# Two-layer streaming trunk with PEER experts: the operands of the gate products change places

## The chip, the cores and the metric

The kernel runs on one core of a Trainium2 chip. The metric is the device time of one execution of the whole program in microseconds; for the kernel before, the median of three runs is 2138.87 us (2137.55 to 2143.28).

The engines named below: PE (TensorE) does the matrix products, a product being a load of weights (the stationary operand) and a MATMUL that streams the moving operand past them into PSUM; DVE (VectorE), ACT (ScalarE) and POOL (GpSimd) work element by element; SP issues the transfers. Each engine has a queue of its own and works through it in order.

## The reference

Two request groups, 256 prompt tokens and 32 sample tokens of width 1024, go through two layers (an RG-LRU block, then a Conformer convolution block). Each layer is followed by a PEER mixer, which is where most of the time goes:

```
q  = h @ w_q                               # 8 heads x 2 halves of 128
s1, s2 = q[..., :half] @ k1.T, q[..., half:] @ k2.T      # 128 keys each
top 16 of s1, top 16 of s2, top 16 of their 256 sums per head
e  = idx1 * 128 + idx2                     # expert, of 16384
g  = softmax(sv)                           # 16 weights per head
z  = gelu(u[e] . h)
out = sum over heads and k of  g * z * v[e]
```

So every token has 8 x 16 = 128 chosen experts, each with a gate weight g.

## The kernel before

For the prompt tokens the kernel does not gather expert rows. It computes z for all 16384 experts with dense products (the up stage, 128 **z items** of 128 experts each), multiplies by a gate matrix that is zero for experts not chosen, and multiplies by all of v (the down stage, 128 v items). One item is one **step** of the stream `run_stream`. The 32 sample tokens do gather their rows, in threads that run beside these stages (`s_up`, L970, and `s_down`, L995).

**A z item** (`z_item`, L922) has these parts, each issued in a fixed step: four transfers load the expert rows (`load`, L925); DVE transposes them in blocks (`prep`, L933, the instruction is L935, two buffers `ut`), two steps ahead; ACT rounds to fp32r (hi, L332) and POOL subtracts for the remainder (lo, L333), one step ahead; PE does 24 products of 256 moving columns (`mm3`, L342), 16 with hi as weights and 8 with lo; a step later, for every second item, ACT applies gelu (L956, or L958 for tokens whose gates are there already, followed on DVE by the multiplication L959). The results go to `gz`, with the expert's low index on the partitions and items by tokens along the rows.

**The gate matrix** of a token is built as a sum of one-hot products. The 128 slots (head, k) of a token lie on the partitions. Slot s contributes its gate at place (idx2, idx1), so the matrix is `onehot(idx2).T @ (onehot(idx1) * g)`. The fp32 gate is split into its power of two (`sexp`) and its mantissa, and the mantissa into two f16 parts (`pmant`, in PSUM, as are the indices `pidx`), so that 16-bit products give the full value.

`gate_ops(g)` (L870) does this for four tokens at a time, 64 **groups** a layer. Its parts:

- `eq` (L878), on DVE: two compares with a ramp (L880, L881) make the one-hot rows `b4` (of idx2) and `one` (of idx1), and two multiplications (L882, L883) make `hi` and `lo` from `one`. All these tiles are 128 x 512 with the four tokens innermost: the row of token j is every fourth element.
- `exps` (L885), on ACT: four scalings (L887) multiply the row of each token in `b4` by its power of two, in place.
- `mm` (L889), on PE: for each token two products (L893), weights `b4[:, :, j]`, moving `hi[:, :, j]` and then `lo[:, :, j]`, summed in one PSUM bank for the four tokens.
- `ev` (L896): DVE multiplies the z values that are there already by the gates (L901), and ACT copies the gates for the items still to come (L904; L906 on DVE for the last few).

**What sets the order.** There is no scheduler: instructions go into the queues in the order in which the program issues them. After the products of each item, `run_threads` (L183) goes through the live threads in order of their start. An operation has a hop, its fourth entry: how many steps after the operation before it, at the least, it may be issued. For a group `eq` and `exps` are issued in the same step, `mm` one step later, `ev` another step later. A "Q" lets one group begin in each step, and a condition keeps a group from starting until the products of the group three before are issued. `hi`, `lo` and `b4` have three sets that groups take in turn, `one` has two. All lie in one scratch tile, `scr`, cut by `four(i, dt)` (L867) into pieces of 256 words. Pieces 0 and 1 held the indices and mantissas on their way to PSUM, and are free by then.

Of the kernel before, what the change touches and what calls it, by code (L numbers as in the profile page):

```python
# [11 lines left out]
F16 = mybir.dt.float16  # L12
BF16 = mybir.dt.bfloat16
I32 = mybir.dt.int32
U32 = mybir.dt.uint32
AF = mybir.ActivationFunctionType
ALU = mybir.AluOpType
# [4 lines left out]
P = 128  # L22
D = 1024
C = 8
NP = 256
# [21 lines left out]
def trunk_kernel(ctx: ExitStack, tc: tile.TileContext, I: dict, O: list):  # L47
    nc = tc.nc
    ctx.enter_context(tc.manual_schedule())
    V, S, G, TE = nc.vector, nc.scalar, nc.gpsimd, nc.tensor  # L50
# [14 lines left out]
    scr = bigp.tile([P, NSCR], F32, name="scr")  # L65
# [6 lines left out]
    def bank(acc=False):  # L72
        if acc:
            return psA.tile([P, 512], F32, tag="acc", name="acc")
        return psB.tile([P, 512], F32, tag="b", name="b")
# [520 lines left out]
    iota4 = scr[:, 3 * NP:4 * NP].bitcast(F16).rearrange("p (i t) -> p i t", t=4)  # L596
    sexp = scr[:, 2 * NP:3 * NP]
# [7 lines left out]
    def peer_items(l, st, x8, sq8, hT8, hp8, rep8, ada_list):  # L605
# [261 lines left out]
        def four(i, dt):  # L867
            return scr[:, i * NP:(i + 1) * NP].bitcast(dt).rearrange("p (i t) -> p i t", t=4)

        def gate_ops(g):  # L870
            t0 = 4 * g
            hi, lo, b4 = [four(4 + 3 * (g % 3) + i, dt) for i, dt in enumerate((F16, F16, BF16))]
            one = four(13 + g % 2, F16)
            tok = slice(t0, t0 + 4)
            s = {}
            row = lambda a: a.unsqueeze(1).to_broadcast([P, P, 4])

            def eq():  # L878
                idx, mant = st["pidx"], st["pmant"]
                V.tensor_tensor(b4, iota4, row(idx[:, 1, tok]), op=ALU.is_equal)  # L880
                V.tensor_tensor(one, iota4, row(idx[:, 0, tok]), op=ALU.is_equal)  # L881
                V.tensor_tensor(hi, one, row(mant[:, 0, tok]), op=ALU.mult)  # L882
                V.tensor_tensor(lo, one, row(mant[:, 1, tok]), op=ALU.mult)  # L883

            def exps():  # L885
                for j in range(4):
                    S.activation(b4[:, :, j], b4[:, :, j], AF.Copy, scale=sexp[:, t0 + j:t0 + j + 1])  # L887

            def mm():  # L889
                s["ps"] = bank(True)  # L890
                for j in range(4):
                    for a in (hi, lo):
                        TE.matmul(s["ps"][:, j * P:(j + 1) * P], b4[:, :, j], a[:, :, j], start=a is hi, stop=a is lo)  # L893
                st["nm"] += 1

            def ev():  # L896
                nz = st["nz"]
                assert st["nt"] == t0
                src = s["ps"].rearrange("p (t i) -> p i t", t=4)
                if nz:  # L900
                    V.tensor_tensor(gz[:, :nz, t0:t0 + 4], gz[:, :nz, t0:t0 + 4], src[:, :nz], op=ALU.mult)  # L901
                if nz < ET:
                    if ET - nz > 10:
                        last.append(lambda: S.copy(gz[:, nz:, t0:t0 + 4], src[:, nz:]))  # L904
                    else:
                        V.tensor_copy(gz[:, nz:, t0:t0 + 4], src[:, nz:])  # L906
                st["nt"] = t0 + 4
                if t0 == NP - 4:
                    for j in range(NS):
                        threads.append(Thread(s_up(j), group=("up%d" % l, 2)))  # L910
            return [("C", 0, lambda: st["nm"] >= g - 2), ("Q", 0, None), ("X", 0, eq, 0), ("X", 0, exps, 0),
                    ("X", 0, mm, 1), ("X", 0, ev, 1)]

        def start_gates():
            for g in range(NP // 4):
                threads.append(Thread(gate_ops(g), group=("gate%d" % l, 5)))
# [53 lines left out]
        def s_up(s):  # L970
            gt = scr[:, (s % 2) * D:(s % 2 + 1) * D]

            def ga():
                if s == 0:
                    nc.sync.dma_start(hs_v, hsave)
                G.indirect_dma_start(out=gt, out_offset=None, in_=Uf,  # L976
                                     in_offset=bass.IndirectOffsetOnAxis(ap=eidx[:, s:s + 1], axis=0))

            def dot():
                V.scalar_tensor_tensor(gt, gt, 1.0, hs_v, op0=ALU.mult, op1=ALU.mult, accum_out=zs[:, s:s + 1])  # L980
            ops = [("R", 1.6, None), ("G", 0.1, ga), ("V", 1.3, dot, 2)]
            if s == NS - 1:
                def act():
                    S.activation(zs, zs, AF.Gelu_apprx_tanh)

                def mid():
                    V.tensor_tensor(zs, zs, gsel, op=ALU.mult)
                    V.tensor_tensor(lz, dmask.unsqueeze(1).to_broadcast([P, NS, NS]),
                                    zs.unsqueeze(2).to_broadcast([P, NS, NS]), op=ALU.mult)
                    for j in range(0, NS, 2):  # L990
                        threads.append(Thread(s_down(j), group=("down%d" % l, 2)))
                ops += [("S", 0.2, act, 2), ("V", 1.4, mid, 2)]
            return ops
# [901 lines left out]
```

## Time and profile before

| | |
|---|---|
| median of 3 runs | 2138.87 us |
| profiled execution, its time | 2135.33 us |
| its span, first to last instruction | 2133.2 us |
| mean granted TensorE clock | 0.989 |
| gate groups of layer 0, about | 431.5 to 671.7 us |
| gate groups of layer 1, about | 1483.6 to 1723.7 us |

A row of the groups of instructions reads: line, engine, operation, written tile <- read tiles, shapes, count | busy us, mean ns of one | idle time of the engine ahead of them, and what ended it. "PEld" are PE's weight loads, which overlap with its products. A row of the waits reads: engine and line that waited <- engine and line waited for: us in all, times, the longest. A row of the stretches reads: the stretch, its length, then for each engine busy us and the number of instructions, the granted clock, the share of the transfer engines in use and the rate. A row of the order of time reads: start, duration from the first start to the last end, engine, line, count.

### The profile page before, as it was taken

Reading aid. Unit: us, or ns where it says so; the run is one execution under the profiler, and the core shown is the slowest. Engines: PE = TensorE matmul, PEld = TensorE weight load, DVE = VectorE, ACT = ScalarE, POOL = GpSimd, SP = SyncE. Lnnn points to the kernel's source line nnn. Section 1 sums busy time; section 2 is a strip of 40 time slices with the busy share of each in tenths; the row PEclk is TensorE's granted clock in tenths of the full one; section 3 lists DMA queues with packets and bytes.
Section 4 is the critical chain, followed back from the end, with each engine's and each line's share of the span. In section 5 each row is a group of like instructions: output and inputs, shape, how many; then the busy total and the mean of one; then the engine's idle time right before and its main releaser. Section 6 shows DMA issues by size and latency. Waiting matters only on the chain.

```text
span 2133.2 us, 38012 instructions
## 1 busy us (share of the span) xinstructions
PE 2048.1 (96%) x13603; PEld 1772.8 (83%) x13603; DVE 1550.8 (73%) x3316; ACT 1127.2 (53%) x1975; POOL 1000.4 (47%) x649
## 2 busy tenths in 40 slices
PE   7988999999999999999999899999999999999997
PEld 4777979999999788777876689989999997777776
DVE  4786569888888787455668755898888887765455
ACT  3654434477776444344443544445877754444444
POOL 4346667856666332110245366877666653211201
PEclk9999999999999999999999999999999999999999
DMA  9756585644445888886676545555444478888863
GB/s 337 261 184 208 153 237 164 179 134 144 139 139 174 304 310 298 283 277 229 237 262 146 169 143 158 173 159 169 148 139 139 134 236 302 296 278 294 277 199 121
DMA packets 311483, 444.44 MB, mean 208 GB/s; under 512 B 29326, under 2 KB 248126, under 8 KB 310782
## 3 DMA queue, kind: packets, MB, share of 16 engines
q1 hardware_dynamic: 292142, 374.73, 55.8%
q0 software_dynamic: 18976, 67.22, 9.0%
q8 instruction: 107, 1.75, 0.4%
q14 instruction: 82, 0.67, 0.1%
q10 hardware_dynamic: 176, 0.07, 0.0%
HBM read 434.19 MB, written 4.87 MB: 206 GB/s over the span
## 4 chain that ended last, share of the span: by engine, by line
PE 70%; DVE 13%; DMA 6%; issue 4%; POOL 4%; ACT 2%; SPq 1%; DVEq 0%; ACTq 0%; POOLq 0%
PE b L342 31%; PE acc L1069 27%; PE acc L893 5%; DVE ut L935 3%; POOL lo L333 3%; DMA raw<-in_peer_v_dram 2%; DMA raw<-in_peer_u_dram 2%; PE b L1013 1%; ACT hi L332 1%; DVE lo L333 1%; PE acc L406 1%; POOL scr L976 1%; DMA scr<-in_peer_u_dram,eidx 1%; PE b L695 1%; PE b L1689 1%
## 5 line engine op out<-in xcount | busy, mean ns | idle before, releaser
L342 PE MATMUL b<-rnd,hi 128*128 128x256 f32 (+1 forms) x5376 | 741.1, 290 | 19.2 <-ACT hi L332 8.4
L333 POOL TENSOR_TENSOR lo<-ut,hi 128x1024 fp32r<-128x1024 f32 x252 | 606.0, 2408 | 287.2 <-ACT hi L332 231.9
L342 PEld LDWEIGHTS b<-rnd,hi 128*128 128x128 f32 x5376 | 684.1, 190 | 43.4 <-ACT hi L332 15.2
L332 ACT CAST hi<-raw 128x1024 fp32r<-128x1024 f32 x336 | 353.1, 1052 | 397.0 <-DMA raw<-in_peer_v_dram 240.5
L1069 PE MATMUL acc<-hi,rnd 128*128 128x512 f32 x2048 | 557.7, 394 | 5.0 <-ACT hi L332 4.8
L333 DVE TENSOR_TENSOR lo<-raw,hi 128x1024 fp32r<-128x1024 f32 x282 | 348.1, 1238 | 257.2 <-PE acc L1069 127.8
L1069 PEld LDWEIGHTS acc<-hi,rnd 128*128 128x128 f32 x2048 | 380.3, 188 | 114.0 <-issue 22.5
L935 DVE STREAM_TRANSPOSE ut<-raw 128x1024 f32<-128x1024 f32 x256 | 317.3, 1240 | 187.8 <-POOL lo L333 93.7
L342 PE MATMUL b<-rnd,lo 128*128 128x256 f32 (+1 forms) x2688 | 387.3, 286 | 12.1 <-POOL lo L333 6.2
L342 PEld LDWEIGHTS b<-rnd,lo 128*128 128x128 f32 x2688 | 351.4, 189 | 17.8 <-POOL lo L333 10.1
L332 ACT CAST hi<-ut 128x1024 fp32r<-128x1024 f32 x256 | 268.4, 1048 | 159.8 <-DVE ut L935 139.2
L1069 PE MATMUL acc<-lo,rnd 128*128 128x512 f32 x1024 | 318.0, 391 | 1.1 <-DVE lo L333 0.8
L887 ACT ACTIVATE scr<-scr 128x128 bf16<-128x128 bf16 x512 | 192.2, 572 | 124.5 <-DVE scr L880 124.5
L1069 PEld LDWEIGHTS acc<-lo,rnd 128*128 128x128 f32 x1024 | 191.0, 188 | 46.4 <-DVE lo L333 6.7
L1003 POOL DMA_INDIRECT big<-in_peer_v_dram,eidx x64 | 62.1, 970 | 271.7 <-PE b L1013 258.6
L333 POOL TENSOR_TENSOR lo<-raw,hi 128x1024 fp32r<-128x1024 f32 x54 | 130.4, 2418 | 114.8 <-PE b L342 59.0
L976 POOL DMA_INDIRECT scr<-in_peer_u_dram,eidx x64 | 86.6, 1353 | 183.4 <-DVE scr L980 182.6
L893 PE MATMUL acc<-scr 128*128 128x128 f16 x1024 | 142.5, 296 | 2.6 <-DVE scr L882 2.5
L893 PEld LDWEIGHTS <-scr 128*128 128x128 bf16 x1024 | 104.1, 118 | 9.8 <-ACT scr L887 3.0
L980 DVE SCALAR_TENSOR_TENSOR scr<-scr 128x1024 f32<-128x1024 f32 x64 | 78.2, 1222 | 36.7 <-DMA scr<-in_peer_u_dram,eidx 35.9
L1044 DVE TENSOR_TENSOR rnd<-big,rnd 128x512 fp32r<-128x512 f32 x128 | 89.9, 702 | 5.5 <-ACT rnd L1043 5.5
L1043 ACT CAST rnd<-big 128x512 fp32r<-128x512 f32 x128 | 78.7, 615 | 5.5 <-PE b L342 5.5
(316 smaller groups left out, 1625.8 us busy)
## 6 DMA issues: line engine op xcount, KB each, us to landing
raw<-in_peer_u_dram SPq DMA_DIRECT2D x1024, 128.0 KB
raw<-in_peer_v_dram SPq DMA_DIRECT2D x256, 512.0 KB
big<-in_ada_w_dram SPq DMA_DIRECT2D x96, 512.0 KB
raw<-in_peer_w_q_dram SPq DMA_DIRECT2D x128, 128.0 KB
raw<-in_cf_w_pw_dram SPq DMA_DIRECT2D x24, 512.0 KB
raw<-in_lru_w_in_dram SPq DMA_DIRECT2D x16, 512.0 KB
raw<-in_lru_w_out_dram SPq DMA_DIRECT2D x8, 512.0 KB
xsave<-big SPq DMA_DIRECT2D x2, 1152.0 KB
```

The costliest lines, as they stand in the source:

```text
L332: S.copy(hi, src)
L333: (G if pool_lo else V).tensor_tensor(lo, src, hi.bitcast(F32), op=ALU.subtract)
L342: TE.matmul(ps, w[wi][:, c * P:(c + 1) * P], a[ai][:, c, :n], start=(start and wi == c == ai == 0), stop=(stop and wi == 1 and c == C - 1))
L887: S.activation(b4[:, :, j], b4[:, :, j], AF.Copy, scale=sexp[:, t0 + j:t0 + j + 1])
L893: TE.matmul(s["ps"][:, j * P:(j + 1) * P], b4[:, :, j], a[:, :, j], start=a is hi, stop=a is lo)
L935: V.transpose(s["ut"].rearrange("p (b e n) -> p e b n", b=8, e=4), s["raw"].rearrange("p (e b n) -> p e b n", e=4, b=8))
L976: G.indirect_dma_start(out=gt, out_offset=None, in_=Uf, in_offset=bass.IndirectOffsetOnAxis(ap=eidx[:, s:s + 1], axis=0))
L980: V.scalar_tensor_tensor(gt, gt, 1.0, hs_v, op0=ALU.mult, op1=ALU.mult, accum_out=zs[:, s:s + 1])
L1003: G.indirect_dma_start(out=gt[j], out_offset=None, in_=Vf, in_offset=bass.IndirectOffsetOnAxis(ap=eidx[:, s + j:s + j + 1], axis=0))
L1043: S.copy(w[0], src)
L1044: V.tensor_tensor(w[1], src, w[0].bitcast(F32), op=ALU.subtract)
L1069: TE.matmul(acc[tt][half], w[a][:, c0:c0 + P], s["w"][b][:, half * 512:(half + 1) * 512], start=(i == 0 and a == 0 and b == 0), stop=(i == ...
```

## The change

In the gate products the two operands change places, and with them the index that each one-hot row stands for, so that the result has the same layout. `b4` is now the one-hot rows of idx1 and `one` those of idx2; `hi` and `lo` (f16, every fourth element) become the weights. The scalings no longer work in place: they read `b4`, still every fourth element, and write a tile `bt` that has the four tokens outermost, so that the row of a token is 128 adjacent bf16 elements; these are the moving operand. `b4` goes to two sets in pieces 0 and 1 of the scratch, `bt` has three sets in pieces 10 to 12. `exps` gets a hop of 1: the scalings of a group are issued one step after its compares, and its products and their use follow a step later than before.

```diff
         def gate_ops(g):
             t0 = 4 * g
-            hi, lo, b4 = [four(4 + 3 * (g % 3) + i, dt) for i, dt in enumerate((F16, F16, BF16))]
+            hi, lo = [four(4 + 2 * (g % 3) + i, F16) for i in range(2)]
+
+            b4 = four(g % 2, BF16)
+            bt = scr[:, (10 + g % 3) * NP:(11 + g % 3) * NP].bitcast(BF16).rearrange("p (t i) -> p t i", t=4)
             one = four(13 + g % 2, F16)
...
             def eq():
                 idx, mant = st["pidx"], st["pmant"]
-                V.tensor_tensor(b4, iota4, row(idx[:, 1, tok]), op=ALU.is_equal)
-                V.tensor_tensor(one, iota4, row(idx[:, 0, tok]), op=ALU.is_equal)
+                V.tensor_tensor(b4, iota4, row(idx[:, 0, tok]), op=ALU.is_equal)
+                V.tensor_tensor(one, iota4, row(idx[:, 1, tok]), op=ALU.is_equal)
                 V.tensor_tensor(hi, one, row(mant[:, 0, tok]), op=ALU.mult)
                 V.tensor_tensor(lo, one, row(mant[:, 1, tok]), op=ALU.mult)
 
             def exps():
                 for j in range(4):
-                    S.activation(b4[:, :, j], b4[:, :, j], AF.Copy, scale=sexp[:, t0 + j:t0 + j + 1])
+                    S.activation(bt[:, j], b4[:, :, j], AF.Copy, scale=sexp[:, t0 + j:t0 + j + 1])
 
             def mm():
                 s["ps"] = bank(True)
                 for j in range(4):
                     for a in (hi, lo):
-                        TE.matmul(s["ps"][:, j * P:(j + 1) * P], b4[:, :, j], a[:, :, j], start=a is hi, stop=a is lo)
+                        TE.matmul(s["ps"][:, j * P:(j + 1) * P], a[:, :, j], bt[:, j], start=a is hi, stop=a is lo)
                 st["nm"] += 1
...
-            return [("C", 0, lambda: st["nm"] >= g - 2), ("Q", 0, None), ("X", 0, eq, 0), ("X", 0, exps, 0),
+            return [("C", 0, lambda: st["nm"] >= g - 2), ("Q", 0, None), ("X", 0, eq, 0), ("X", 0, exps, 1),
                     ("X", 0, mm, 1), ("X", 0, ev, 1)]
```

## The prediction

> **What bounds the kernel now.** I read the page's busy times and chain first, then the stretches in which the gate products run, then who waits for whom in them, and last the order of time of single instructions.
>
> ```profile
> PE 2048.1 (96%) x13603; PEld 1772.8 (83%) x13603; DVE 1550.8 (73%) x3316; ACT 1127.2 (53%) x1975; POOL 1000.4 (47%) x649
> PE 70%; DVE 13%; DMA 6%; issue 4%; POOL 4%; ACT 2%; SPq 1%; DVEq 0%; ACTq 0%; POOLq 0%
> ```
>
> TensorE carries 70% of the chain. 96% is an average over stages, so here are the two stretches that hold the gate products (layer 0, layer 1), and of the first one its beginning and its end:
>
> ```profile
> core 0: us, PE busy (x) PEld busy (x) DVE busy (x) ACT busy (x) POOL busy (x), PEclk, DMA share, GB/s
> 431.50:671.70 240.20, 239.41 (x2017) 235.37 (x2018) 206.03 (x416) 183.12 (x442) 152.20 (x64) 1.00 0.47 141
> 431.50:465.50 34.00, 33.21 (x275) 32.17 (x276) 27.74 (x60) 27.74 (x66) 21.65 (x9) 1.00 0.48 147
> 636.00:671.70 35.70, 35.70 (x304) 35.16 (x303) 32.24 (x64) 24.45 (x60) 21.34 (x10) 1.00 0.45 134
> 1483.60:1723.70 240.10, 239.39 (x2017) 235.31 (x2017) 206.19 (x414) 182.62 (x441) 152.73 (x64) 1.00 0.47 141
> ```
>
> In both, PE has no idle time to speak of (239.4 of 240.2 us), at full granted clock (1.00), with DMA at half use. DVE stands next, at 82% at the beginning (27.74 of 34.00) and 90% at the end (32.24 of 35.70). The waits of the first stretch say the same:
>
> ```profile
> POOL lo L333 <- ACT hi L332: 89.5, 62, 6.0
> ACT scr L887 <- DVE scr L880: 56.1, 62, 1.7
> DVE ut L935 <- POOL lo L333: 29.3, 31, 1.2
> DVE big L959 <- ACT b L958: 1.4, 2, 1.1
> PEld L893 <- ACT scr L887: 1.5, 2, 1.3
> PE acc L893 <- DVE scr L882: 1.3, 1, 1.3
> ```
>
> PE waits some 3 us in all. POOL, ACT and DVE wait a great deal, each for another, and none of it reaches PE. So only what PE does itself can shorten these 480 us; anything else counts only if it becomes the next bound.
>
> **What a gate product costs PE.** One z item of the up stage without gates, then one with a gate group, from the order of time (start, duration, engine, line):
>
> ```profile
> 379.73 1.11 PE L342 MATMUL b<-rnd,lo 128*128 128x256 f32 x8
> 380.68 2.03 PE L342 MATMUL b<-rnd,hi 128*128 128x256 f32 x16
> 382.54 1.11 PE L342 MATMUL b<-rnd,lo 128*128 128x256 f32 x8
> ...
> 504.95 1.11 PE L893 MATMUL acc<-scr 128*128 128x128 f16 x8
> 505.82 2.14 PE L342 MATMUL b<-rnd,hi 128*128 128x256 f32 x16
> 507.79 1.11 PE L342 MATMUL b<-rnd,lo 128*128 128x256 f32 x8
> 508.74 1.11 PE L893 MATMUL acc<-scr 128*128 128x128 f16 x8
> ```
>
> Without gates the period is 382.54 - 379.73 = 2.81 us, or 0.117 us for each of the 24 products of 256 moving columns. With a gate group it is 508.74 - 504.95 = 3.79 us. The eight gate products thus take 0.98 us, 0.122 us each. They have only 128 moving columns, yet take as long as products of 256. How time goes with columns is seen in the down stage, with 512 columns:
>
> ```profile
> 900.79 1.07 PE L1069 MATMUL acc<-hi,rnd 128*128 128x512 f32 x4
> 901.70 0.62 PE L1069 MATMUL acc<-lo,rnd 128*128 128x512 f32 x2
> 902.15 1.07 PE L1069 MATMUL acc<-hi,rnd 128*128 128x512 f32 x4
> ```
>
> Six products take 902.15 - 900.79 = 1.36 us, 0.227 each. From 256 to 512 columns that is 0.110 us more, 0.00043 us a column, so 128 adjacent columns come to 0.117 - 0.055 = 0.062 us. A gate product takes twice that. Two things set it apart. Its moving operand (a[:, :, j]) has every fourth element of a row, and its weights (b4[:, :, j]) do too. Which is the slow one? The weight loads give a hint:
>
> ```profile
> L342 PEld LDWEIGHTS b<-rnd,hi 128*128 128x128 f32 x5376 | 684.1, 190 | 43.4 <-ACT hi L332 15.2 <-issue 6.8 <-DVE rnd L491 5.5
> L893 PE MATMUL acc<-scr 128*128 128x128 f16 x1024 | 142.5, 296 | 2.6 <-DVE scr L882 2.5
> L893 PEld LDWEIGHTS <-scr 128*128 128x128 bf16 x1024 | 104.1, 118 | 9.8 <-ACT scr L887 3.0
> ```
>
> A z product lives with a load of 190 ns every 117 ns, so loads overlap with products. The gate's load takes 118 ns, 72 ns less, and by the same overlap would allow a product every 117 - 72 = 45 ns. So I take the moving operand to be the slow one: each of its spread columns costs two.
>
> **The change part by part.** (1) *Operands swapped.* 1024 products and 1024 loads stay. The moving operand becomes bt[:, j], 128 adjacent elements; the weights become hi or lo, spread as b4 was, in two-byte elements too. If the spread moving operand is the cause, a product costs 0.062 us. The ends: 0.045 us (the bound by the load) and 0.122 us (the load, or the spread weights, hold it where it is). I take 0.062, the nearest row's slope, because the loads of 190 ns speak against the upper end. A group then costs 8 x 0.062 + 0.04 = 0.54 us; the 0.04 is what a group now costs above eight z products (0.98 - 8 x 0.117). PE's step: 2.81 + 0.54 = 3.35 us.
>
> The Trainium skill, "TensorE: Matmul & The Clock Gate", section "Back-to-back issue gap", gives about 81 ns as what a stream of load-and-product pairs with 128 columns sustains. By that the group would be 0.69 us, the step 3.50 us and the gain 37 us. No run here has such a stream of adjacent 16-bit columns.
>
> (2) *The next bound.* With PE at 3.35 us, what does DVE need? In the first stretch it waits 29.3 + 1.4 us; 240.2 - 30.7 = 209.5 us over 240.2 / 3.79 = 63.4 steps is 3.31 us a step. It grows along the stage, since L901 and L959 treat more of each row: busy 0.82 x 3.79 = 3.09 us at the beginning, 0.90 x 3.79 = 3.42 at the end, and some 0.05 of short gaps. The change takes nothing from DVE: four compares and products a group stay. So PE sets the step in the first half and DVE in the second; the mean of the larger is 3.38 us. Every second step carries an L959 on DVE and the others none, so I add 0.04: **3.42 us**.
>
> (3) *Scalings one step later, out of place.* Now ACT stands behind L880 for 56.1 us in the stretch, with the next weight cast (L332, hi) queued behind it, for which POOL waits 89.5 us, for whose lo the transpose on DVE (L935) waits 29.3 us. After the change the scalings of a group stand in ACT's queue one step behind its compares, so this row goes, POOL's lo starts earlier and most of DVE's 29.3 us should go. On PE that is worth nothing today; it is what lets DVE run at 3.31 to 3.47 instead of 3.79. If it stayed, DVE would hold the step at 3.79.
>
> ```profile
> L887 ACT ACTIVATE scr<-scr 128x128 bf16<-128x128 bf16 x512 | 192.2, 572 | 124.5 <-DVE scr L880 124.5
> L551 ACT ACTIVATE big<-big,modA 32x256 f32<-32x256 f32 x32 | 16.1, 504 | 0.6
> L1657 ACT ACTIVATE big<-big,scr 128x318 f32<-128x318 f32 x9 | 4.4, 553 | 0.0
> ```
>
> A scaling with a per-partition factor on adjacent elements costs 504 ns for 256 and 553 for 318, hence about 400 for 128. The spread one costs 572. Written adjacent but read spread, it lies between 400 and 572. Either way it is off the path: ACT needs 183.1 / 63.4 = 2.89 us a step at most.
>
> New waits: the first compare writes b4, of which there are now two, and must wait for the scalings of two groups before. They stand in ACT's queue one step earlier, and ACT has half a microsecond a step to spare; behind that compare would stand DVE's transpose. The rewriting of hi and lo waits for the products of three groups before, now one step earlier instead of two. But the multiplication L901 that stands ahead of it on DVE waits for the same products, so it adds nothing. No DMA moves; loads of the table come sooner with the transposes, at 47% DMA use.
>
> (4) *One step of latency.* The last group ends one z item later.
>
> ```profile
> 1723.65 1.11 PE L893 MATMUL acc<-scr 128*128 128x128 f16 x8
> ...
> 1733.06 2.03 PE L342 MATMUL b<-rnd,hi 128*128 128x256 f32 x16
> ```
>
> ```profile
> L1013 PE MATMUL b<-big,scr x256: 592/605/617, 845.9 to 2049.9; 128*32 128x512 f32 x128
> L1069 PE MATMUL acc<-lo,rnd x1024: 387/389/504, 692.3 to 2121.6; 128*128 128x512 f32 x171
> ```
>
> Z items still follow it (layer 1 here), and the sample's chain, which starts with it, has its last products (L1013) 72 us before the down stage ends. So the delay is covered. Uncovered it would be 3.4 us a layer.
>
> Sum: (3.79 - 3.42) x 64 steps x 2 layers = 47 us. The profiled execution took 2135.3 us (span 2133.2), giving 2088; the median shown is 3.5 us higher. I forecast **2089 us**; its own range runs from 3.31 us a step (DVE's mean, PE never in the way: 61 us less, 2074) to 3.57 (2107).
>
> **Rivals.**
> *No change.* The load or the spread weights set the 0.122 us, and the swap leaves both. The step stays 3.79 and the time 2135 to 2139. For it: gate loads last 118 ns and products come every 118 to 122, as if each load were waited for. Against it: the 190 ns loads at 117 ns. By the Trainium skill, "Advanced Engine Details and Errata", section "SBUF Cachelines", lines are 16 bytes and two hits on a line suffice for full speed; two-byte elements 8 bytes apart give two, so a spread moving operand would be free and this rival right. The trace shows twice the time, but not which operand's it is.
>
> *DVE or its ring takes over.* The transpose keeps waiting for POOL. The ring of two ut buffers (1.24 transpose, 1.05 cast, 2.41 lo, rows below) needs 4.70 us for two steps, far below 6.8, so only the queues' order could hold it. If half of today's 0.48 us wait a step stays, the step is about 3.6 and the time 2135 - 0.19 x 128 = 2111.
>
> ```profile
> L935 DVE STREAM_TRANSPOSE ut<-raw 128x1024 f32<-128x1024 f32 x64 | 79.4, 1241 | 29.3 <-POOL lo L333 29.3
> L332 ACT CAST hi<-ut 128x1024 fp32r<-128x1024 f32 x65 | 67.9, 1046 | 0.0
> L333 POOL TENSOR_TENSOR lo<-ut,hi 128x1024 fp32r<-128x1024 f32 x64 | 154.3, 2410 | 92.2 <-ACT hi L332 89.5 <-PE b L342 1.8 <-ACT big L956 0.9
> ```
>
> *Slower.* The spread f16 weights load slower than the spread bf16 ones and become PE's bound. It decides once a load occupies more than the 0.122 us of now. If it stood unhidden at the 190 ns of an f32 load, a group would cost 8 x 0.07 = 0.54 us more: 128 x 0.54 = 70 us, 2205. Against it: both are two-byte, and nothing in the rows depends on which.
>
> *More than forecast.* The load's bound of 0.045 us and a DVE that gives way: below 2070.
>
> **How the numbers follow.** Forecast 0.67; no change 0.18; DVE's ring 0.07; slower 0.05; below 2070 0.03. A measurement of this kernel can tell about 0.3%, 6.4 us, from no change. Faster: 0.67 + 0.07 + 0.03 = 0.77; same 0.18; slower 0.05. 2074 to 2107 alone would leave a third out, so the range reaches over the ring to no change: 2070 to 2141.
>
> **What would show it.** Right: starts of gate products 0.06 us apart; PE's step near 3.4 us, with PE idle for the first time in the second half of the stretches and DVE above 95% there; no row of L887 waiting for L880; DVE's wait for POOL mostly gone; scalings of 400 to 572 ns; all the gain in the two stretches. Wrong: gate products still 0.12 apart (the cause was the load), a longer load row for f16, or DVE idle beside an idle PE (a ring I have not priced).

## The result, and the profile after

The changed kernel takes 2076.64 us (median of 4 runs, 2070.87 to 2089.57), against 2139.53 us for the kernel before in the same comparison: a ratio of 0.9722, 95% interval 0.9701 to 0.9743, some 60 us less. The forecast was 2089 us, 47 us less. The profiled execution has a span of 2077.7 us.

Busy times and chain of the page, changed kernel:

```profile
PE 1996.1 (96%) x13603; PEld 1724.9 (83%) x13603; DVE 1543.2 (74%) x3316; ACT 1115.1 (54%) x1973; POOL 1003.8 (48%) x650
PE 70%; DVE 12%; issue 6%; DMA 5%; POOL 5%; ACT 2%; SPq 0%; DVEq 0%; POOLq 0%; ACTq 0%
```

PE's 96% and its 70% of the chain have not moved. A share can't show the change; PE has 52 us less work, and the program is shorter by about as much. The two stretches of the gate products (columns as before: stretch, length, busy us of PE, weight loads, DVE, ACT, POOL), with the end of the first:

```profile
437.00:648.80 211.80, 211.80 (x2027) 209.05 (x2026) 202.57 (x412) 175.40 (x434) 153.64 (x65) 1.00 0.53 161
612.00:648.00 36.00, 36.00 (x343) 35.56 (x342) 34.85 (x70) 28.33 (x68) 26.16 (x11) 1.00 0.53 157
1465.90:1677.80 211.90, 211.90 (x2027) 209.11 (x2025) 202.54 (x413) 175.44 (x437) 153.89 (x65) 1.00 0.53 161
```

From the first gate product to the last one it was 240.9 us in both; it is now 211.8 in both, 58 us less together. PE still has no idle time, even at the end, where DVE is 97% busy (34.85 of 36.00). One step in PE's order of time:

```profile
561.06 0.64 PE L896 MATMUL acc<-scr 128*128 128x128 bf16 x8
561.51 2.12 PE L342 MATMUL b<-rnd,hi 128*128 128x256 f32 x16
563.47 1.11 PE L342 MATMUL b<-rnd,lo 128*128 128x256 f32 x8
564.42 0.64 PE L896 MATMUL acc<-scr 128*128 128x128 bf16 x8
```

The step is 564.42 - 561.06 = 3.36 us (3.353 on average in layer 0, 3.355 in layer 1), where it was 3.79. Eight gate products span 0.64 us from the first start to the last end, and one lasts 0.22 us, so their starts are (0.64 - 0.22 - 0.03) / 7 = 0.056 us apart; the 0.03 is a longer gap after the first. The groups of the changed lines, and the waits of the first stretch:

```profile
L890 ACT ACTIVATE scr<-scr 128x128 bf16<-128x128 bf16 x512 | 169.8, 409 | 0.1
L896 PE MATMUL acc<-scr 128*128 128x128 bf16 x1024 | 81.9, 223 | 0.0
L896 PEld LDWEIGHTS <-scr 128*128 128x128 f16 x1024 | 61.9, 116 | 5.6
```

```profile
POOL lo L333 <- PE b L342: 40.5, 43, 1.0
ACT big L959 <- PE b L342: 21.2, 29, 1.1
...
DVE big L962 <- ACT b L961: 5.7, 17, 0.4
...
DVE ut L938 <- POOL lo L333: 0.6, 2, 0.4
```

ACT no longer waits for the first compare (it was 56.1 us), DVE hardly for POOL (0.6 us, it was 29.3), and now POOL and ACT wait mostly for PE, the engine that sets the pace.

### The profile page after: what moved, and what is told of

The parts are those of the page before. It is cut to its first block, busy times and chain, and to the rows that moved or that the text cites. A ratio compares the mean times of both kernels' runs of the same rounds, so it can differ in the third digit from the quotient of the medians.

```text
span 2077.7 us, 38019 instructions
## 1 busy us (share of the span) xinstructions
PE 1996.1 (96%) x13603; PEld 1724.9 (83%) x13603; DVE 1543.2 (74%) x3316; ACT 1115.1 (54%) x1973; POOL 1003.8 (48%) x650
## 4 chain that ended last, share of the span: by engine, by line
PE 70%; DVE 12%; issue 6%; DMA 5%; POOL 5%; ACT 2%; SPq 0%; DVEq 0%; POOLq 0%; ACTq 0%
PE b L342 33%; PE acc L1072 27%; DVE ut L938 3%; PE acc L896 3%; POOL lo L333 3%; DMA raw<-in_peer_u_dram 2%; POOL scr L979 2%; PE b L1016 1%; DVE acc L781 1%; ACT hi L332 1%; DMA big<-in_ada_w_dram 1%; DVE lo L333 1%; PE acc L406 1%; DMA raw<-in_peer_v_dram 1%; PE b L695 1%
## 5 line engine op out<-in xcount | busy, mean ns | idle before, releaser
L890 ACT ACTIVATE scr<-scr 128x128 bf16<-128x128 bf16 x512 | 169.8, 409 | 0.1
L959 ACT ACTIVATE big<-b 128x512 f32<-128x512 f32 (+32 forms) x123 | 59.9, 487 | 69.7 <-PE b L342 69.4
L896 PE MATMUL acc<-scr 128*128 128x128 bf16 x1024 | 81.9, 223 | 0.0
```

The costliest lines, as they stand in the source:

```text
L890: S.activation(bt[:, j], b4[:, :, j], AF.Copy, scale=sexp[:, t0 + j:t0 + j + 1])
L896: TE.matmul(s["ps"][:, j * P:(j + 1) * P], a[:, :, j], bt[:, j], start=a is hi, stop=a is lo)
```

## The experiments

**Each half alone.** First the swap without the delay:

```diff
-            return [("C", 0, lambda: st["nm"] >= g - 2), ("Q", 0, None), ("X", 0, eq, 0), ("X", 0, exps, 1),
+            return [("C", 0, lambda: st["nm"] >= g - 2), ("Q", 0, None), ("X", 0, eq, 0), ("X", 0, exps, 0),
```

> The operands swapped and the scalings out of place, but issued in the same step as the compares. Theory (PE alone paces the stretch, and DVE needs only some 3.25 us a step): PE's step stays 3.35 us, gate products 0.056 us apart, time as the changed kernel's, 2070 to 2090 us; DVE's waits for POOL come back in part but reach PE nowhere. Rival (the delay is what lets DVE keep up): ACT again waits for the first compare, hi and lo come late, DVE waits about 0.48 us a step as before, the step goes to 3.6 to 3.79 us and the time to 2105 to 2135 us, with PE idle in front of products that wait for hi or lo.

Measured: 2126.69 us, ratio to the kernel before 0.9946 (0.9923 to 0.9968). My theory fell: the swap alone brings 11 us of the 60. Waits of its first stretch, then its order of time from one transpose to the one two steps on:

```profile
ACT scr L890 <- DVE scr L883: 61.9, 61, 6.5
DVE ut L938 <- POOL lo L333: 26.3, 30, 1.2
PEld b L342 <- POOL lo L333: 14.2, 31, 0.5
PE b L342 <- POOL lo L333: 7.3, 24, 0.3
...
566.03 1.25 DVE L938 STREAM_TRANSPOSE ut<-raw 128x1024 f32<-128x1024 f32 x1 [0.83 <-POOL lo L333]
...
567.25 0.45 DVE L962 TENSOR_TENSOR big<-b,big 128x280 f32<-128x280 f32 x1
...
567.61 0.54 DVE L904 TENSOR_TENSOR big<-big,acc 128x376 f32<-128x376 f32 x1
568.07 0.41 DVE L883 TENSOR_TENSOR scr<-scr,acc 128x512 bf16<-128x512 f16 x1
...
568.51 1.32 ACT L890 ACTIVATE scr<-scr 128x128 bf16<-128x128 bf16 x4 [1.30 <-DVE scr L883]
...
569.89 1.05 ACT L332 CAST hi<-ut 128x1024 fp32r<-128x1024 f32 x1
...
571.02 2.40 POOL L333 TENSOR_TENSOR lo<-ut,hi 128x1024 fp32r<-128x1024 f32 x1 [2.00 <-ACT hi L332]
...
573.45 1.25 DVE L938 STREAM_TRANSPOSE ut<-raw 128x1024 f32<-128x1024 f32 x1 [0.82 <-POOL lo L333]
```

Read it as a ring. The transpose is followed on DVE by two multiplications and the first compare. ACT waits 1.30 us for that compare, scales, and only then casts hi: its input had been there since 567.28 us, the end of the transpose, but the cast stands behind the scalings in the queue. POOL subtracts, and only then is one of the two `ut` buffers free for the transpose two steps on. The ring is 573.45 - 566.03 = 7.42 us, 3.71 a step, and PE waits for lo. No engine in it is full: in this stretch of 234.2 us DVE is busy for 203.6, ACT for 175.1 and POOL for 151.4.

The same ring in the kernel before:

```profile
558.26 1.25 DVE L935 STREAM_TRANSPOSE ut<-raw 128x1024 f32<-128x1024 f32 x1 [0.94 <-POOL lo L333]
...
560.32 0.41 DVE L880 TENSOR_TENSOR scr<-scr,acc 128x512 bf16<-128x512 f16 x1
560.66 0.41 DVE L881 TENSOR_TENSOR scr<-scr,acc 128x512 f16<-128x512 f16 x1
560.77 1.50 ACT L887 ACTIVATE scr<-scr 128x128 bf16<-128x128 bf16 x4 [1.27 <-DVE scr L880]
...
562.29 1.04 ACT L332 CAST hi<-ut 128x1024 fp32r<-128x1024 f32 x1
...
563.41 2.42 POOL L333 TENSOR_TENSOR lo<-ut,hi 128x1024 fp32r<-128x1024 f32 x1 [2.11 <-ACT hi L332]
...
565.86 1.25 DVE L935 STREAM_TRANSPOSE ut<-raw 128x1024 f32<-128x1024 f32 x1 [0.96 <-POOL lo L333]
```

565.86 - 558.26 = 7.60 us for two steps. PE's own need was 2 x 3.79 = 7.58. Two bounds of nearly the same length stood there side by side, and PE was the one that set the step: its groups follow each other at 3.79 us in every step but the first, just as in the next kernel, where the ring is broken. The ring is shorter than PE's two steps at first and longer at the end, and a lead bridges this: between the end of a subtraction on POOL and the products that use its lo lie 0.05 us at the beginning of the stretch, 3.3 in the middle and 1.2 to 1.7 at the end. Once the swap takes 0.43 us a step from PE, the ring is what remains; there the lead is down to 0.05 us in every second step.

Second, the delay without the swap:

```diff
-            return [("C", 0, lambda: st["nm"] >= g - 2), ("Q", 0, None), ("X", 0, eq, 0), ("X", 0, exps, 0),
+            return [("C", 0, lambda: st["nm"] >= g - 2), ("Q", 0, None), ("X", 0, eq, 0), ("X", 0, exps, 1),
```

> The kernel before with the scalings issued one step later, nothing else. Theory: PE is full at 3.79 us a step, so the time does not move (ratio 0.997 to 1.003), though ACT's wait for the first compare (56 us in a stretch) and DVE's wait for POOL (29 us) go. Rival (part of the gain is the delay's): 5 to 15 us faster.

Measured: 2127.78 us, ratio 0.996 (0.9938 to 0.9983): some 9 us faster, as the rival had it. Its stretch, and one of its waits:

```profile
436.30:675.90 239.60, 239.60 (x2027) 236.12 (x2025) 206.31 (x412) 184.66 (x436) 153.99 (x65) 1.00 0.47 143
...
DVE ut L935 <- POOL lo L333: 1.2, 2, 0.8
```

The ring is gone (1.2 us of waits for POOL), PE is full, and the step stays 3.79 us. The halves give 11 and 9 us; together they give 60. Of the 9 us that the delay gives alone, the stretches show some 3 (239.6 against 240.9 each: the first step takes 3.78 us where it took 5.13, the others are as they were); the rest lies outside them.

A second profile of the kernel before was taken to see how much of that is chance:

> The kernel before once more, for a second profile: how much the stages differ from run to run where nothing was changed. Theory: the gate stretches are 240.9 us again to 0.5 us; the down stages (380.2 and 382.9 us) differ by several us, and these differences are as large as what the delay alone seemed to gain there. Rival: the down stages come out the same to 1 us, and the delay's gain outside the gate stretches is real.

Measured: 2141.19 us; stretches of 240.8 us both. The down stage took 385.4 us in layer 0, where the first profile had 380.2, and 382.9 in layer 1, as the first. So differences of 5 us arise there with nothing changed, and 2.5 us ahead of the first gate product (434.1 against 431.6 us). The two kernels with a spread moving operand below contain the delay too and took 2125.7 and 2128.36 us, so the gain in time came again; where the 6 us outside the stretches arise is left open.

**Is it the ring?** Two of the four scalings are left out of the swap without the delay, and the products of the other two tokens use the rows that are there:

```diff
-                for j in range(4):
+                for j in range(2):
                     S.activation(bt[:, j], b4[:, :, j], AF.Copy, scale=sexp[:, t0 + j:t0 + j + 1])
...
-                        TE.matmul(s["ps"][:, j * P:(j + 1) * P], a[:, :, j], bt[:, j], start=a is hi, stop=a is lo)
+                        TE.matmul(s["ps"][:, j * P:(j + 1) * P], a[:, :, j], bt[:, j % 2], start=a is hi, stop=a is lo)
```

> The swap without the delay, with two of the four scalings of a group left out (the products of tokens 2 and 3 of a group use the rows of tokens 0 and 1, so gates are wrong there; all 8 products stay). Theory (a ring holds the swap without the delay: transpose, multiplications and first compare on DVE, the scalings behind it on ACT, the cast behind those, POOL's subtraction, the transpose two steps on; 7.42 us for two steps, of which the scalings are 1.32): two scalings fewer take 0.61 us off, the ring is 6.8, the step 3.40, the time 2127 - 126 x 0.31 = 2088, give or take 7. Rival (the ring is not the bound; PE waits for something else): step 3.6 to 3.7, time over 2115.

Measured: 2086.97 us against a forecast of 2088, 40 us less than with four scalings. ACT is far from full (137.2 of 214.9 us), and PE's work is the same, so 0.6 us of ACT's time in every step can count only as a link of the ring. Two subtractions on POOL, two steps apart, and two parts of the first stretch:

```profile
564.26 2.40 POOL L333 TENSOR_TENSOR lo<-ut,hi 128x1024 fp32r<-128x1024 f32 x1 [1.44 <-ACT hi L332]
...
571.14 2.41 POOL L333 TENSOR_TENSOR lo<-ut,hi 128x1024 fp32r<-128x1024 f32 x1 [1.44 <-ACT hi L332]
...
465.20:616.00 150.80, 150.72 (x1438) 148.57 (x1437) 142.78 (x290) 97.12 (x225) 107.28 (x45) 1.00 0.53 157
616.00:648.80 32.80, 32.39 (x302) 31.15 (x301) 31.82 (x63) 18.81 (x44) 21.60 (x9) 1.00 0.50 150
```

Here the ring takes 571.14 - 564.26 = 6.88 us; the starts of the subtractions give its length all along the first stretch. It grows, since DVE's multiplications treat more and more of each row:

| us for two steps | 2nd pair of steps | 16th | 30th | PE's need |
|---|---|---|---|---|
| kernel before | 7.12 | 7.58 | 7.77 | 7.58 |
| swap alone | 7.00 | 7.36 | 7.73 | 6.71 |
| swap alone, two scalings | 6.38 | 6.76 | 7.13 | 6.71 |

In the kernel before PE holds the ring to its own pace in the middle. Without the delay, two scalings fewer shorten the ring by 0.60 to 0.62 us everywhere; 0.61 was forecast. The mean step is 3.40 us, as forecast too, but not because each step is: after a first step of 4.46 us PE is full for some fifty steps (3.353 us), for it gets ahead while the ring is short, and waits in the last twelve, where the mean is above 3.5. That the mean of these came out at 3.40 is in part luck.

**Which operand is the slow one.** The swapped kernel with its moving operand spread again:

```diff
-            bt = scr[:, (10 + g % 3) * NP:(11 + g % 3) * NP].bitcast(BF16).rearrange("p (t i) -> p t i", t=4)
+            bt = four(10 + g % 3, BF16)
...
-                        TE.matmul(s["ps"][:, j * P:(j + 1) * P], a[:, :, j], bt[:, j], start=a is hi, stop=a is lo)
+                        TE.matmul(s["ps"][:, j * P:(j + 1) * P], a[:, :, j], bt[:, :, j], start=a is hi, stop=a is lo)
```

> The changed kernel, but the scaled rows written with the four tokens innermost, so that the moving operand is spread again (every fourth 16-bit element, 8 bytes apart); operands swapped as in the change, weights unchanged. Theory (the spread moving operand costs two cycles a column): gate products 0.118 us apart again, PE's step 3.79 us, time 2135, give or take 8. Rival (what counted is which operand is the weights, or f16 against bf16): products 0.056 apart, step 3.35, time 2077.

And the kernel before, with its roles and its spread moving operand, but adjacent weights (scaled out of place, one step later):

```diff
-                    S.activation(b4[:, :, j], b4[:, :, j], AF.Copy, scale=sexp[:, t0 + j:t0 + j + 1])
+                    S.activation(bt[:, j], b4[:, :, j], AF.Copy, scale=sexp[:, t0 + j:t0 + j + 1])
...
-                        TE.matmul(s["ps"][:, j * P:(j + 1) * P], b4[:, :, j], a[:, :, j], start=a is hi, stop=a is lo)
+                        TE.matmul(s["ps"][:, j * P:(j + 1) * P], bt[:, j], a[:, :, j], start=a is hi, stop=a is lo)
```

> The kernel before with roles unchanged, but its weights (the scaled rows) written adjacent, out of place and one step later; hi and lo still stream spread. Theory (the weights' spread costs nothing): products 0.118 us apart, step 3.79 us, time 2135 to 2143 as before, though the weights are now adjacent. Rival (the spread load held the products): products 0.06 apart, step 3.35, time 2077.

Measured: 2125.7 and 2128.36 us, somewhat below what was expected, for both contain the delay, which alone gives 2127.78; their steps are 3.788 and 3.767 us, where 3.79 was expected. Their groups, and a gate group of each in PE's order of time, the spread moving operand first:

```profile
L896 PE MATMUL acc<-scr 128*128 128x128 bf16 x1024 | 142.2, 296 | 0.0
L896 PEld LDWEIGHTS <-scr 128*128 128x128 f16 x1024 | 103.9, 118 | 6.7
...
562.41 1.11 PE L896 MATMUL acc<-scr 128*128 128x128 bf16 x8
```

```profile
L895 PE MATMUL acc<-scr 128*128 128x128 f16 x1024 | 139.2, 292 | 0.0
L895 PEld LDWEIGHTS <-scr 128*128 128x128 bf16 x1024 | 102.1, 112 | 5.8
...
560.91 1.09 PE L895 MATMUL acc<-scr 128*128 128x128 f16 x8
```

Both have the products as far apart as the kernel before, 0.116 and 0.114 us, (1.11 - 0.296) / 7 and (1.09 - 0.292) / 7, whichever operand is which, in f16 or bf16, with spread weights or adjacent ones. What they share is the spread moving operand.

**How far apart is too far.** The moving operand with two tokens innermost (4 bytes from column to column), and with room for eight (16 bytes):

```diff
-            bt = scr[:, (10 + g % 3) * NP:(11 + g % 3) * NP].bitcast(BF16).rearrange("p (t i) -> p t i", t=4)
+            bt = scr[:, (10 + g % 3) * NP:(11 + g % 3) * NP].bitcast(BF16).rearrange("p (u i v) -> p u v i", u=2, v=2)
...
-                    S.activation(bt[:, j], b4[:, :, j], AF.Copy, scale=sexp[:, t0 + j:t0 + j + 1])
+                    S.activation(bt[:, j // 2, j % 2], b4[:, :, j], AF.Copy, scale=sexp[:, t0 + j:t0 + j + 1])
...
-                        TE.matmul(s["ps"][:, j * P:(j + 1) * P], a[:, :, j], bt[:, j], start=a is hi, stop=a is lo)
+                        TE.matmul(s["ps"][:, j * P:(j + 1) * P], a[:, :, j], bt[:, j // 2, j % 2], start=a is hi, stop=a is lo)
```

The second takes more room, so that `bt` has two sets there and `one` a single one:

```diff
-            bt = scr[:, (10 + g % 3) * NP:(11 + g % 3) * NP].bitcast(BF16).rearrange("p (t i) -> p t i", t=4)
-            one = four(13 + g % 2, F16)
+            bt = scr[:, (10 + 2 * (g % 2)) * NP:(12 + 2 * (g % 2)) * NP].bitcast(BF16).rearrange("p (i t) -> p t i", t=8)
+            one = four(14, F16)
```

> The changed kernel with two tokens innermost in the scaled rows: the moving operand has every second 16-bit element, 4 bytes apart. Theory (a column costs by the bytes that the read passes over, 4 bytes being what an f32 column has): products 0.056 us apart as with adjacent elements, step 3.35, time 2077. Rival (any gap between 16-bit elements halves the rate): 0.118 apart, step 3.79, time 2135.

> The changed kernel with room for eight tokens innermost, four of them used: the moving operand has every eighth 16-bit element, 16 bytes apart. Theory (the cost grows with the bytes passed over): 0.22 us apart or so, a group 1.8 us, step 4.65, time 2245. Rival (one price for any spread element): 0.118 apart, step 3.79, time 2135.

Measured: 2075.41 and 2247.34 us. Gate products of each in PE's order of time:

```profile
561.24 0.66 PE L896 MATMUL acc<-scr 128*128 128x128 bf16 x8
...
564.62 0.66 PE L896 MATMUL acc<-scr 128*128 128x128 bf16 x8
```

```profile
563.50 2.01 PE L896 MATMUL acc<-scr 128*128 128x128 bf16 x8
565.15 1.07 PE L342 MATMUL b<-rnd,hi 128*128 128x256 f32 x6
```

At 4 bytes a group takes nearly what adjacent elements take (0.66 against 0.64 us; the stretch 214.2 against 211.8, which is 0.005 us more a product, so 0.060 or so). At 8 bytes a product is 0.114 to 0.118, at 16 bytes (2.01 - 0.41) / 7 = 0.229 us. From 4 to 8 and from 8 to 16 bytes the price doubles with the distance, from 2 to 4 it hardly changes; other distances were not run. PE waits for no other engine in these stretches (busy 214.2 of 214.2 us at 4 bytes, 297.3 of 297.3 at 16).

**The next bound.** The changed kernel without the gate products of lo:

```diff
-                    for a in (hi, lo):
-                        TE.matmul(s["ps"][:, j * P:(j + 1) * P], a[:, :, j], bt[:, j], start=a is hi, stop=a is lo)
+                    TE.matmul(s["ps"][:, j * P:(j + 1) * P], hi[:, :, j], bt[:, j], start=True, stop=True)
```

> The changed kernel without the gate products of the low mantissa parts (lo is still computed on DVE, but not multiplied), so four products a group instead of eight; the gates lose the low half of their mantissas. PE's step would be 3.353 - 4 x 0.056 = 3.13 us. Theory (DVE is the next bound, close above): the step stops at DVE's need, 3.2 to 3.3 us, with PE idle 0.1 to 0.2 us a step, and the time is 2077 - 128 x 0.1 = 2064, give or take 6. Rival (DVE has room left): the step is 3.13, PE full, time 2049.

Measured: 2059.96 us, inside what the theory had (2064, give or take 6). Its first stretch, up to near its end and the rest:

```profile
438.70:600.00 161.30, 161.30 (x1441) 159.12 (x1440) 159.09 (x332) 142.88 (x357) 124.40 (x52) 1.00 0.57 170
600.00:637.80 37.80, 37.44 (x329) 36.50 (x328) 37.42 (x77) 30.06 (x74) 26.73 (x12) 1.00 0.53 154
```

Up to 600 us PE is full at 3.14 us a step, as the rival had it, with DVE 98.6% busy (159.09 of 161.30); only in the last steps, where DVE's work has grown, does PE wait, and the mean is 3.16 us. So DVE's need is some 3.16 us a step on the mean, not the 3.31 that I had worked out, and the changed kernel is 0.2 us a step away from it. At the end of the stretch nothing of this room is left: DVE's transposes at 618.04 and 624.82 us, two steps apart with no wait between them, make 3.39 us a step. In the changed kernel those at 608.13 and 614.86 us make 3.37, a little more than PE's 3.353; PE does not feel it, because the subtraction still ends 3.0 us ahead of the products that use it.

**Run to run, and a version that pays less.** The changed kernel was run again:

> The changed kernel once more, to see what of its time moves from run to run. Theory: the two gate stretches take 211.7 us each again, to 0.5 us, and the differences between runs (2071 to 2090 us) lie in the down stages, where transfers are in use at over 80%. Rival: the stretches themselves vary.

Measured: 2074.31 us, ratio 0.9698 (0.9665 to 0.9732); stretches of 211.6 and 211.8 us, down stages of 384.3 and 379.0 us, where the first profile had 388.5 and 377.0. The stretches are the same, as the theory had it. Of the 5.1 us between the two profiled executions, though, only 2.2 lie in the down stages; 2.9 lie ahead of the first gate product, which starts at 434.1 us here and at 437.0 there.

A group costs PE 3.353 - 2.81 = 0.54 us, though eight products are 0.45. Most of the rest lies at one place: the second z product behind a group starts 0.20 us after the first, elsewhere 0.117. So the last kernel pays the ends of a group once for two groups. Beside the lines shown, b4 and one have one set each (pieces 0 and 1), bt lies in pieces 12 to 14, and the compare for b4 comes last of the four:

```diff
-            hi, lo = [four(4 + 2 * (g % 3) + i, F16) for i in range(2)]
+            hi, lo = [four(4 + 2 * (g % 4) + i, F16) for i in range(2)]
...
-                    ("X", 0, mm, 1), ("X", 0, ev, 1)]
+                    ("X", 0, mm, 2 - g % 2), ("X", 0, ev, 1)]
```

> The changed kernel, but with the products of two groups issued together in every second step (even groups held one step longer; hi and lo in four sets, one in one, b4 in one and compared last). A group costs PE 8 x 0.056 = 0.45 us and some 0.09 at its two ends, where a weight load has too short a product to hide behind. Theory (the ends are paid once for two groups): the step falls by 0.045 us on average, 126 x 0.045 = 6 us, ratio to the kernel before 0.967 against the change's 0.970 to 0.972. Rival (DVE, now with two multiplications in one step and none in the next and a single b4, falls out of step): no gain, or 5 to 20 us slower than the changed kernel, with DVE waiting for ACT's scalings.

Measured: 2066.6 us, ratio 0.9677 (0.9658 to 0.9696). In its order of time:

```profile
563.07 1.11 PE L342 MATMUL b<-rnd,lo 128*128 128x256 f32 x8
564.02 1.08 PE L896 MATMUL acc<-scr 128*128 128x128 bf16 x16
564.91 2.13 PE L342 MATMUL b<-rnd,hi 128*128 128x256 f32 x16
566.87 1.11 PE L342 MATMUL b<-rnd,lo 128*128 128x256 f32 x8
```

Sixteen products stand together, and PE stays full. Of the kernels that compute the whole result it is the fastest of the study. The mean step, from the first products to the last, is 206 / 62 = 3.32 us against 3.353, about 4 us in all, where 6 were expected; the intervals of the ratios overlap with the changed kernel's second one, so that it beats the changed kernel is likely but not shown.

## Why the prediction was right or wrong

**PE's new step: right, to 0.01 us.** The slope of the rows gave 0.062 us a product and 0.54 a group; measured are 0.056 and 0.54. The product was a little cheaper and the ends of a group a little dearer than what I took over from the old group (0.09 against 0.04), so that the sum is this close because two errors cancel.

**The slow operand: right.** The hint of the 190 ns loads was good: spreading the moving operand alone brings all of the 0.118 back, making the weights adjacent brings no more than 0.02 us of a step. With this the no-change rival falls, and with it the rule of the Trainium skill that it drew on, as it was read there ("Advanced Engine Details and Errata", section "SBUF Cachelines"): elements 8 bytes apart give two hits on a 16-byte line, yet cost twice. So does the slower rival: the spread f16 load takes 116 to 118 ns, as the bf16 one did. The 81 ns of the Trainium skill ("TensorE: Matmul & The Clock Gate", section "Back-to-back issue gap") for a stream with 128 columns was also not what bound here; it was 56.

**The next bound: wrong, and this is the 11 us that were missing.** The step was put at 3.42 us because DVE was to need 3.31 on average and 3.47 at the end. The term that failed is that need: the stretch less DVE's waits for POOL and ACT. But work and waits are not two separate parts. Adjacent instructions of DVE overlap (L881 starts 0.34 us after L880, which lasts 0.41), and one that waits has nothing to overlap with. So the busy time itself shrank with the waits: 206.03 / 63.4 = 3.25 us a step before, (159.09 + 37.42) / 63 = 3.12 in the kernel without the products of lo, which gives DVE the same work (some 0.04 of the difference is where the cuts fall: 416 / 63.4 = 6.56 instructions a step in the one, 408 / 63 = 6.48 in the other). That the need grows along the stretch was right; at the end it is 3.39, not 3.47, and the lead covers what is above PE's step. The 0.04 for the uneven L962 (L959 before) does not show either: PE's steps in layer 0 are all 3.35 us. The sum has a slip too: by its own ends, 3.14 and 3.47, DVE would pass 3.35 at two thirds of the stretch and not at half, and the mean of the larger is 3.37, not 3.38. The difference of 3.42 to 3.353 is 8.5 us over 126 steps; the stalls of the first groups, which I had not counted (5.13 against 3.79 us for the first step of a stretch), make up 2 to 3 more.

**The delay: right in what it does, mis-weighed in the rivals.** Part 3 said that without it DVE would stay at 3.79 us; without it the step was 3.71, and the gain 11 us instead of 60. But the ring was priced by its three engine times, 4.70 us, with a remark that only the order of the queues could hold it. That order puts the compare and the scalings inside, and the ring was 7.1 to 7.8 us long already in the kernel before. I took the 0.48 us of DVE's wait for slack that had no length of its own. In the experiment on the swap alone I forgot my own remark and expected nothing from the delay.

**The new waits and the step of latency: right.** No wait for b4, hi or lo appears. The first gate products start at 437.0 us instead of 431.6 (434.1 in the second profile of either kernel, so this start varies by some 3 us), and in return fewer z items are left after the last group: from it to the first v item it is 14.2 us, where it was 18.5. The scalings cost 409 ns, near the lower of the ends named. PE idle in the second half of the stretches, which I expected to see, did not come.

## What to carry to other kernels

Follow the waits that do not reach the bounding engine round until they close: if they form a ring, write down its length with everything that stands in between in each queue, and compare it with the bounding engine's step before you make that engine faster. Here both were about 7.6 us for two steps, so each half of the change gave about 10 us and both together some 60. A lead built up where the ring is short hides it where it is long, so take its length at the beginning and at the end of the stage, not at one place. And lay a matmul's moving operand out adjacent, or put the spread one on the weights' side, where its load hides behind the products before it.

## What the runs showed of the hardware

- A moving operand of 16-bit elements 2, 4, 8 and 16 bytes apart gives a product of 128 columns every 0.056, 0.060, some 0.117 and 0.229 us: of these distances, 4 bytes costs nearly nothing more, and 8 and 16 double it each.
- Spread weights cost next to nothing beside products of this length: loads of 118 ns spread and 112 adjacent in the same place, and steps of 3.79 and 3.77 us. Beside products 0.056 us apart the spread loads take 116 ns.
- Scalings on ACT from a spread to an adjacent row of 128 take 409 ns, spread to spread 572 (four in a row overlap and take 1.32 and 1.50 us together), and with the written elements 16 bytes apart 1042:

```profile
L890 ACT ACTIVATE scr<-scr 128x128 bf16<-128x128 bf16 x512 | 339.7, 1042 | 44.3 <-PE acc L896 44.3
```

Why the last is so slow (the write itself, or the reads of PE beside it) was not tried.
